# The inverse root of the LayerNorms on GpSimd beside VectorE's first product

## The chip, the cores and the metric

The kernel runs on one core of a Trainium2 chip. A core has a matmul engine (TensorE, PE in the profile), VectorE (DVE), ScalarE (ACT), GpSimd (POOL) and an engine that here only issues loads (SyncE, SP). Each engine takes its instructions in the order in which they stand in its own queue and waits on semaphores for the others. The metric is the time of one execution on the device, in microseconds (us); lower is better.

## The reference

Two transformer blocks of two layers each run one after the other on 256 tokens of width 1024, in float32. The first block normalises with RMS norms. The change concerns the second block only, whose residual stream passes four LayerNorms in each layer:

```python
def _layer_norm(x, g, b):
    xf = x.astype(jnp.float32)
    mu = jnp.mean(xf, -1, keepdims=True)
    var = jnp.mean(jnp.square(xf - mu), -1, keepdims=True)
    return ((xf - mu) * lax.rsqrt(var + LN_EPS) * g + b).astype(x.dtype)
...
    for l in range(DEPTH):          # DEPTH = 2
        x = _layer_norm(a * x + 0.5 * _swiglu(x, ffn1_w1[l], ...), ln1_g[l], ln1_b[l])
        mix = _token_mixing(x, w_in[l], ...)
        x = _layer_norm(a * x + mix, ln2_g[l], ln2_b[l])
        x = _layer_norm(a * x + _cross_attention(x, mem, ...), ln3_g[l], ln3_b[l])
        x = _layer_norm(a * x + 0.5 * _swiglu(x, ffn2_w1[l], ...), ln4_g[l], ln4_b[l])
```

Every product with a weight is a 128x512 matmul chain; to reach float32 accuracy each operand is split into a rounded part (hi) and a rest (lo), and three products are added.

## The kernel before

The tokens are two halves of 128 rows, `x0` (m = 0) and `x1` (m = 1), kept in SBUF. A weight tile is loaded by SP (tiles `raw`), cast to its hi part by ACT (line 329), and its lo part is made by DVE, raw minus hi (line 320, 1024 or 512 columns, both operands in SBUF).

A norm is made by `update` for one half. In order: the residual sum `x = a*x + acc` in two 512-column halves (line 657, `acc` in PSUM), the statistics of each half (line 661), their aggregate (line 666, giving mean and variance in `mv`), the inverse root `rsqrt` on a 128x1 column, and for each 512-column half the first product `(x - mean) * g` (line 679) and the second `x * r + b` (line 681). `rsqrt` has no table: it is an integer estimate and two polynomial steps, eight small VectorE instructions (lines 598, 599, 593, 601, 602, 593, 604, 605), each on the result of the one before.

The normed half is then turned by PE, in two groups of four 128x128 transposes (line 423), into PSUM; from there ACT copies the hi part (line 579) and DVE makes the lo part (line 580, one operand in PSUM). Those are the operands of the next matmuls (line 417).

How the halves are overlapped: `leave` runs the last products of a stage for m = 0 first, so that the norm of `x0` can run on DVE while PE does the products for m = 1; then it transposes `x0`. `gemm_first` begins the next stage with the first six weight tiles (`AHEAD`) for m = 0 while the norm of `x1` runs; then `arrive` ends that norm and transposes `x1`, and the m = 1 products follow. `hasten` gives the norm's instructions a high priority, and a list scheduler then fixes the order of each engine's queue; which other instructions stand between the steps of a norm is its result. The inverse roots of the RMS norms and of the small norms inside the token mixing use the same `rsqrt`.

Of the kernel before, what the change touches and what calls it, by code (L numbers as in the profile page):

```python
# [15 lines left out]
I32 = mybir.dt.int32  # L16
AF = mybir.ActivationFunctionType
ALU = mybir.AluOpType
AX = mybir.AxisListType

P = 128
# [8 lines left out]
LN_EPS = 1e-5  # L30
# [232 lines left out]
class Build:  # L263
# [321 lines left out]
    def rsqrt(self, var, n, eps):  # L585
# [19 lines left out]
        nc.vector.tensor_scalar(y, y, -0.5 * c2 ** 3, None, op0=ALU.mult)  # L605
        return y

    def fetch(self, dst, src):

        i = self.nc.gpsimd.dma_start(dst, src)  # L610
        if self.order is not None:
            self.after(i, self.recent[0])
# [34 lines left out]
    def update(self, m, acc, a, kind):  # L647

        nc, x = self.nc, self.x[m]
        st, mv = self.t("sm", [P, 32]), self.t("sm", [P, 32])  # L650
        halves = [slice(0, 512), slice(512, 1024)]
        for i, c in enumerate(halves):
            if acc is not None:
                if a is None:
                    ins = nc.vector.tensor_add(x[:, c], x[:, c], acc[i])  # L655
                else:
                    ins = nc.vector.scalar_tensor_tensor(x[:, c], x[:, c], a, acc[i], op0=ALU.mult, op1=ALU.add)  # L657
                if m == 1 and i == ORDER:
                    self.after(ins, self.done)
            if kind is not None:  # L660
                nc.vector.bn_stats(st[:, 6 * i:6 * i + 6], x[:, c])  # L661
            yield
        self.h[m] = x
        if kind is None:
            return
        nc.vector.bn_aggr(mv[:, :2], st[:, :12].rearrange("p (a b) -> p a b", b=6))
        if kind[0] == "rms":
            nc.vector.scalar_tensor_tensor(mv[:, 2:3], mv[:, 0:1], mv[:, 0:1], mv[:, 1:2], op0=ALU.mult, op1=ALU.add)
            r = self.rsqrt(mv[:, 2:3], 1, RMS_EPS)
            self.h[m] = self.t("b4", [P, 1024])  # L670
        else:
            r = self.rsqrt(mv[:, 1:2], 1, LN_EPS)
        yield
        for i, c in enumerate(halves):
            if kind[0] == "rms":
                self.done = nc.vector.scalar_tensor_tensor(self.h[m][:, c], x[:, c], r, kind[1][:, c],  # L676
                                                           op0=ALU.mult, op1=ALU.mult)
            else:
                nc.vector.scalar_tensor_tensor(x[:, c], x[:, c], mv[:, 0:1], kind[1][:, c],  # L679
                                               op0=ALU.subtract, op1=ALU.mult)  # L680
                self.done = nc.vector.scalar_tensor_tensor(x[:, c], x[:, c], r, kind[2][:, c],  # L681
                                                           op0=ALU.mult, op1=ALU.add)
            if kind[0] == "last":
                nc.sync.dma_start(self.a["out"][m * P:m * P + P, c], x[:, c])
            yield
# [1208 lines left out]
```

## Time and profile before

| | us |
|---|---|
| median of 3 runs | 2223.34 (2222.77 to 2224.21) |
| the profiled execution | 2224.18 |
| its span | 2222.4 |
| PE busy | 2186.5 |
| DVE busy | 1521.3 |
| ACT busy | 1078.4 |
| POOL busy | 113.7 |

The granted clock of PE is 0.999 over the span. The span is the time from the first to the last instruction of the profiled execution; the rest of its time lies around it. Busy shares tell how loaded an engine is, not what the end waits for; for that the chain and the waits are read, and then the timeline of the stretch in question. In a timeline a row with a count (x2, x8) stands for several instructions in a row, with the time from the first one's start to the last one's end, and consecutive instructions overlap a little.

### The profile page before, as it was taken

To read this page: it belongs to the slowest core of one execution; us is meant where nothing else is said; L and a number is where in the kernel's file an instruction comes from. 1 tells how busy PE (TensorE), PEld (TensorE's weight loads), DVE (VectorE), ACT (ScalarE), POOL (GpSimd) and SP (SyncE) were. 2 spreads that over 40 slices of the span, in tenths; PEclk is the share of its full clock that TensorE was granted. 3 is DMA by queue.
4 is the path that set the end of the run, shared out by engine and by line. 5 is a ranking of instruction groups with operands and counts; after the bars stand their busy time and mean duration, and the time that the engine had idled before them with its cause. 6 is when DMAs were issued, how large, how long until landed. Compare 5 with 4: busy or idle time off the path is not lost.

```text
span 2222.4 us, 30617 instructions
## 1 busy us (share of the span) xinstructions
PE 2186.5 (98%) x11454; PEld 1849.9 (83%) x11454; DVE 1521.3 (68%) x2456; ACT 1078.4 (49%) x1681; POOL 113.7 (5%) x191
## 2 busy tenths in 40 slices
PE   7999999999999999999999999999999999999998
PEld 6878888978888888889888888888888988897886
DVE  7677457778555555888877765575568887778555
ACT  5664344584444444456653444444435665444442
POOL 1000001000000000023000000000000310000000
PEclk9999999999999999999999999999999999999999
DMA  7355455445565555454556455555645444754561
GB/s 263 122 171 182 179 206 171 166 134 170 181 214 188 185 208 202 158 185 152 162 180 217 157 185 208 199 172 184 243 142 197 169 152 152 235 182 152 183 243 48
DMA packets 114709, 399.91 MB, mean 180 GB/s; under 512 B 13056, under 2 KB 13728, under 8 KB 114560
## 3 DMA queue, kind: packets, MB, share of 16 engines
q1 hardware_dynamic: 107712, 374.30, 48.7%
q0 software_dynamic: 6848, 23.66, 3.2%
q8 instruction: 90, 1.47, 0.3%
q14 instruction: 59, 0.48, 0.1%
HBM read 396.85 MB, written 1.05 MB: 179 GB/s over the span
## 4 chain that ended last, share of the span: by engine, by line
PE 86%; DVE 9%; ACT 3%; issue 2%; DMA 1%; SPq 0%; POOL 0%; DVEq 0%; ACTq 0%
PE ps L417 82%; PE ps L423 4%; DVE b L320 2%; DVE b L580 1%; DVE sm L661 1%; DVE x L679 1%; ACT b L329 0%; DVE x L657 0%; DVE x L681 0%; ACT b L579 0%; DVE sm L593 0%; DMA raw<-in_w_in_dram 0%; ACT b L1501 0%; DVE x L655 0%; ACT b L1553 0%
## 5 line engine op out<-in xcount | busy, mean ns | idle before, releaser
L417 PE MATMUL ps<-b,b 128*128 128x512 f32 (+7 forms) x10412 | 2088.6, 362 | 6.0 <-DVE b L320 2.4
L417 PEld LDWEIGHTS ps<-b,b 128*128 128x128 f32 (+2 forms) x10412 | 1734.3, 187 | 317.5 <-issue 10.9
L320 DVE TENSOR_TENSOR b<-raw,b 128x1024 fp32r<-128x1024 f32 (+3 forms) x738 | 843.4, 1179 | 47.8 <-PE ps L417 27.8
L329 ACT CAST b<-raw 128x1024 fp32r<-128x1024 f32 (+3 forms) x738 | 718.2, 1020 | 209.2 <-PE ps L417 135.8
L579 ACT CAST b<-ps 128x512 fp32r<-128x512 f32 (+2 forms) x188 | 101.1, 571 | 396.3 <-PE ps L423 310.7
L580 DVE TENSOR_TENSOR b<-ps,b 128x512 fp32r<-128x512 f32 (+2 forms) x188 | 118.8, 662 | 194.0 <-ACT b L579 193.3
L583 DVE SCALAR_TENSOR_TENSOR b<-ps,b 128x512 fp32r<-128x512 f32 (+1 forms) x64 | 39.1, 652 | 257.4 <-ACT b L582 257.4
L582 ACT ACTIVATE b<-ps 128x512 fp32r<-128x512 f32 (+1 forms) x64 | 33.1, 569 | 338.7 <-PE ps L423 338.7
L423 PE MATMUL ps<-cst,b 128*128 128x128 f32 (+1 forms) x810 | 106.9, 274 | 13.2 <-DVE b L676 11.5
L423 PEld LDWEIGHTS ps<-cst,b 128*128 128x128 f32 (+1 forms) x810 | 93.9, 140 | 25.4 <-DVE b L676 11.7
L610 POOL DMA_DIRECT2D b<-in_rows_dram x55 | 29.7, 543 | 1362.2 <-PE ps L417 899.3
L1553 ACT ACTIVATE b<-b,sm 128x128 f32<-128x128 f32 (+1 forms) x128 | 56.6, 446 | 8.0 <-DVE sm L828 7.8
L795 DVE TENSOR_TENSOR b<-b,ps 128x512 f32<-128x512 f32 (+1 forms) x48 | 30.8, 641 | 38.0 <-PE ps L417 36.7
L888 DVE TENSOR_TENSOR b<-ps,b 128x512 f32<-128x512 f32 x32 | 22.1, 689 | 27.1 <-PE ps L417 27.0
L890 ACT ACTIVATE b<-b 128x512 f32<-128x512 f32 x32 | 20.0, 629 | 41.8 <-DVE b L888 41.8
L661 DVE BATCH_NORM_STATS2 sm<-x 128x6 f32<-128x512 f32 x48 | 32.7, 688 | 4.1 <-DMA x<-in_x_dram 3.7
L1573 DVE TENSOR_TENSOR b<-b,sm 128x512 f32<-128x512 f32 x48 | 34.2, 740 | 0.3
L784 ACT ACTIVATE b<-ps 128x512 f32<-128x512 f32 x32 | 19.3, 604 | 27.4 <-PE ps L417 27.4
L793 ACT ACTIVATE b<-ps 128x512 f32<-128x512 f32 (+1 forms) x48 | 26.9, 561 | 10.4 <-PE ps L417 5.2
L794 DVE SCALAR_TENSOR_TENSOR b<-b,ps 128x512 f32<-128x512 f32 (+1 forms) x48 | 30.5, 636 | 0.0
L785 DVE SCALAR_TENSOR_TENSOR b<-ps,b 128x512 f32<-128x512 f32 x32 | 21.8, 685 | 12.5 <-ACT b L784 12.5
L871 DVE SCALAR_TENSOR_TENSOR b<-b,ps 128x512 f32<-128x512 f32 x32 | 21.7, 684 | 11.3 <-PE ps L417 11.3
(170 smaller groups left out, 744.6 us busy)
## 6 DMA issues: line engine op xcount, KB each, us to landing
raw<-in_ffn_w_dram SPq DMA_DIRECT2D x248, 512.0 KB, 5.6
raw<-in_w_in_dram SPq DMA_DIRECT2D x184, 512.0 KB, 4.7
raw<-in_w_up_dram SPq DMA_DIRECT2D x64, 512.0 KB, 5.2
raw<-in_w_down_dram SPq DMA_DIRECT2D x64, 512.0 KB, 5.0
b<-in_rows_dram POOLq DMA_DIRECT2D x19, 512.0 KB, 7.3
raw<-in_w_out_dram SPq DMA_DIRECT2D x16, 512.0 KB, 4.2
raw<-in_ffn_w_dram SPq DMA_DIRECT2D x32, 256.0 KB, 2.9
raw<-in_w_o_dram SPq DMA_DIRECT2D x16, 512.0 KB, 5.4
```

Source lines behind the costliest of these rows:

```text
L320: i = self.nc.vector.tensor_sub(lo[:, :n], r[:, :n], hi[:, :n].bitcast(F32))
L329: self.nc.scalar.copy(hi[:, :n], r[:, :n])
L417: i = self.nc.tensor.matmul(out, lhsT, rhs, start=start, stop=stop, skip_group_check=True)
L423: i = self.nc.tensor.transpose(out, in_, self.ident[:k, :k])
L579: nc.scalar.copy(hi, src)
L580: nc.vector.tensor_sub(lo, src, hi.bitcast(F32))
L582: nc.scalar.activation(hi, src, AF.Copy, scale=scale)
L583: nc.vector.scalar_tensor_tensor(lo, src, scale, hi.bitcast(F32), op0=ALU.mult, op1=ALU.subtract)
L661: nc.vector.bn_stats(st[:, 6 * i:6 * i + 6], x[:, c])
L795: nc.vector.tensor_mul(h[:, :w], r[:, :w], pss[1])
L1553: nc.scalar.activation(p[:, i], p[:, i], AF.Exp, scale=-1.0, bias=nm[:, at + i:at + i + 1], accum_out=den[:, at + i:at + i + 1])
L1573: e.tensor_mul(p, p, rinv[:, at:at + n].unsqueeze(2).broadcast_to((P, n, w)))
```

## The change

A second function makes the inverse root with the same eight steps on GpSimd, all as `tensor_scalar` on a 128x1 column; five of them take one or both scalars from a column in SBUF. `update` calls it for LayerNorms; the RMS norms keep the VectorE version. What follows it in the file moves down by 15 lines, so line 666 becomes 681, line 679 becomes 694 and line 681 becomes 696.

```diff
+    def rsqrt1(self, var, eps):
+
+        e = self.nc.gpsimd
+        c0, c1, c2 = 1.94246764, -1.3888181, 0.44639636
+        v, y, t = (self.t("sm", [P, 32])[:, :1] for _ in range(3))
+        e.tensor_scalar(v, var, eps, None, op0=ALU.add)
+        e.tensor_scalar(y.bitcast(I32), v.bitcast(I32), -0.5, 1596981248.0, op0=ALU.mult, op1=ALU.add)
+        e.tensor_scalar(t, y, y, v, op0=ALU.mult, op1=ALU.mult)
+        e.tensor_scalar(t, t, c1 / c2, t, op0=ALU.add, op1=ALU.mult)
+        e.tensor_scalar(y, t, c0 / c2, y, op0=ALU.add, op1=ALU.mult)
+        e.tensor_scalar(t, y, y, v, op0=ALU.mult, op1=ALU.mult)
+        e.tensor_scalar(y, t, -3 / c2 ** 2, y, op0=ALU.add, op1=ALU.mult)
+        e.tensor_scalar(y, y, -0.5 * c2 ** 3, None, op0=ALU.mult)
+        return y
...
         else:
-            r = self.rsqrt(mv[:, 1:2], 1, LN_EPS)
+            r = self.rsqrt1(mv[:, 1:2], LN_EPS)
```

In the order of the instructions 128 rows (16 norms of 8) leave DVE and 128 come to POOL. In the rows below a name is a tile with a running number (`sm` a small column, `b4` and `b2` SBUF tiles, `ps` a PSUM tile, `raw` a weight as loaded).

On POOL, the eight steps for `x1` of the first LN1, which stand right behind the eight for `x0`:

```order
L613 TENSOR_SCALAR sm_1678_8000<-sm_1670_7957 128x1
L614 TENSOR_SCALAR sm_1679_8001<-sm_1678_8000 128x1
L615 TENSOR_SCALAR sm_1680_8002<-sm_1679_8001,sm_1678_8000 128x1
L616 TENSOR_SCALAR sm_1680_8002<-sm_1680_8002 128x1
L617 TENSOR_SCALAR sm_1679_8001<-sm_1680_8002,sm_1679_8001 128x1
L618 TENSOR_SCALAR sm_1680_8002<-sm_1679_8001,sm_1678_8000 128x1
L619 TENSOR_SCALAR sm_1679_8001<-sm_1680_8002,sm_1679_8001 128x1
L620 TENSOR_SCALAR sm_1679_8001<-sm_1679_8001 128x1
```

Each step reads what the one before wrote; the first waits for the aggregate on DVE, and line 696 on DVE waits for the last.

On DVE, the same norm (`x1`, first LN1), before:

```order
L666 BN_AGGR sm_1670_7957<-sm_1669_7956 128x2
L679 SCALAR_TENSOR_TENSOR x1_83<-x1_83,sm_1670_7957,b4_1591_7604 128x512 x2
L598 TENSOR_SCALAR sm_1678_8000<-sm_1670_7957 128x1
L1071 TENSOR_TENSOR b2_1691_8058<-ps_1684_8021,b2_1362_6473 128x440
L599 TENSOR_SCALAR sm_1679_8001<-sm_1678_8000 128x1
L593 SCALAR_TENSOR_TENSOR sm_1680_8002<-sm_1679_8001,sm_1678_8000 128x1
L633 TENSOR_TENSOR b2_1698_8082<-b2_1691_8058,cst_81 128x32
L634 TENSOR_TENSOR b2_1699_8083<-b2_1691_8058,cst_81 128x16
L601 SCALAR_TENSOR_TENSOR sm_1680_8002<-sm_1680_8002 128x1
L635 TENSOR_TENSOR b2_1699_8083<-b2_1691_8058,cst_81 128x16
```

and after:

```order
L681 BN_AGGR sm_1670_7957<-sm_1669_7956 128x2
L694 SCALAR_TENSOR_TENSOR x1_83<-x1_83,sm_1670_7957,b4_1591_7604 128x512 x2
L696 SCALAR_TENSOR_TENSOR x1_83<-x1_83,sm_1679_8001,b4_1592_7606 128x512 x2
L320 TENSOR_TENSOR b4_1682_8016<-raw_1650_7858,b4_1681_8015 128x1024
L320 TENSOR_TENSOR b4_1686_8029<-raw_1651_7860,b4_1685_8028 128x1024
L1086 TENSOR_TENSOR b2_1691_8058<-ps_1684_8021,b2_1362_6473 128x440
L320 TENSOR_TENSOR b4_1689_8041<-raw_1654_7872,b4_1688_8040 128x1024
L598 TENSOR_SCALAR sm_1694_8065<-sm_1693_8062 128x2
L648 TENSOR_TENSOR b2_1698_8082<-b2_1691_8058,cst_81 128x32
```

The bias sum of the next stage (line 1071, 1086 after) and the rotary operations, which stood between the steps, now stand behind both products and the first conversions; nothing stands between line 694 and line 696.

On DVE at the first LN3, around the norm of `x1`, before:

```order
L681 SCALAR_TENSOR_TENSOR x0_82<-x0_82,sm_2468_11773,b4_2448_11711 128x512 x2
L657 SCALAR_TENSOR_TENSOR x1_83<-x1_83,ps_2445_11707 128x512
L580 TENSOR_TENSOR b4_2450_11714<-ps_2472_11809,b4_2449_11713 128x4x128
L661 BN_STATS sm_2470_11799<-x1_83 128x6
L580 TENSOR_TENSOR b4_2452_11716<-ps_2473_11816,b4_2451_11715 128x4x128
L666 BN_AGGR sm_2471_11800<-sm_2470_11799 128x2
L320 TENSOR_TENSOR b4_2465_11758<-raw_2406_11523,b4_2464_11757 128x1024
L679 SCALAR_TENSOR_TENSOR x1_83<-x1_83,sm_2471_11800,b4_2447_11709 128x512 x2
L598 TENSOR_SCALAR sm_2478_11845<-sm_2471_11800 128x1
L320 TENSOR_TENSOR b4_2475_11832<-raw_2425_11603,b4_2474_11831 128x1024
L599 TENSOR_SCALAR sm_2479_11846<-sm_2478_11845 128x1
L320 TENSOR_TENSOR b4_2482_11857<-raw_2428_11621,b4_2481_11856 128x1024
```

and after:

```order
L696 SCALAR_TENSOR_TENSOR x0_82<-x0_82,sm_2468_11773,b4_2448_11711 128x512 x2
L672 SCALAR_TENSOR_TENSOR x1_83<-x1_83,ps_2446_11708 128x512
L672 SCALAR_TENSOR_TENSOR x1_83<-x1_83,ps_2445_11707 128x512
L676 BN_STATS sm_2470_11799<-x1_83 128x6 x2
L580 TENSOR_TENSOR b4_2450_11714<-ps_2472_11809,b4_2449_11713 128x4x128
L681 BN_AGGR sm_2471_11800<-sm_2470_11799 128x2
L580 TENSOR_TENSOR b4_2452_11716<-ps_2473_11816,b4_2451_11715 128x4x128
L694 SCALAR_TENSOR_TENSOR x1_83<-x1_83,sm_2471_11800,b4_2447_11709 128x512 x2
L696 SCALAR_TENSOR_TENSOR x1_83<-x1_83,sm_2479_11846,b4_2448_11711 128x512 x2
L320 TENSOR_TENSOR b4_2465_11758<-raw_2406_11523,b4_2464_11757 128x1024
```

The conversions stood before and between the steps of the norm; now all of them stand behind its second products.

On PE at the first LN4, from the second group of `x1`'s transposes (`ps_2810`) on, before:

```order
L423 MATMUL ps_2810_13460<-cst_81,x1_83 128x128 x4
L417 MATMUL ps_2811_13467<-b4_2756_13213,b4_2749_13197 128x512
L417 MATMUL ps_2811_13467<-b4_2757_13214,b4_2749_13197 128x512
L417 MATMUL ps_2811_13467<-b4_2756_13213,b4_2749_13197 128x512
L417 MATMUL ps_2811_13467<-b4_2757_13214,b4_2749_13197 128x512
L417 MATMUL ps_2821_13510<-b4_2770_13265,b4_2749_13197 128x512
L417 MATMUL ps_2821_13510<-b4_2771_13266,b4_2749_13197 128x512
L417 MATMUL ps_2821_13510<-b4_2770_13265,b4_2749_13197 128x512
L417 MATMUL ps_2821_13510<-b4_2771_13266,b4_2749_13197 128x512
L417 MATMUL ps_2808_13440<-b4_2794_13393,b4_2751_13199 128x512
L417 MATMUL ps_2808_13440<-b4_2793_13392,b4_2751_13199 128x512
L417 MATMUL ps_2808_13440<-b4_2794_13393,b4_2751_13199 128x512
```

and after:

```order
L423 MATMUL ps_2810_13460<-cst_81,x1_83 128x128 x4
L417 MATMUL ps_2808_13440<-b4_2793_13392,b4_2751_13199 128x512
L417 MATMUL ps_2811_13467<-b4_2756_13213,b4_2749_13197 128x512
L417 MATMUL ps_2811_13467<-b4_2757_13214,b4_2749_13197 128x512
L417 MATMUL ps_2811_13467<-b4_2756_13213,b4_2749_13197 128x512
L417 MATMUL ps_2811_13467<-b4_2757_13214,b4_2749_13197 128x512
L417 MATMUL ps_2821_13510<-b4_2770_13265,b4_2749_13197 128x512
L417 MATMUL ps_2821_13510<-b4_2771_13266,b4_2749_13197 128x512
L417 MATMUL ps_2821_13510<-b4_2770_13265,b4_2749_13197 128x512
L417 MATMUL ps_2811_13467<-b4_2756_13213,b4_2750_13198 128x512 x2
L417 MATMUL ps_2811_13467<-b4_2759_13225,b4_2749_13197 128x512
L417 MATMUL ps_2811_13467<-b4_2760_13226,b4_2749_13197 128x512
```

The first matmul on `b4_2750`, the lo part that line 580 makes from the transposed `x1`, stands behind 14 matmuls before and behind 8 after (`b4_2749` is the hi part); six on `ps_2808` moved behind it.

## Rows read from the trace of the kernel before

**Rows 1.** The page: busy shares of the engines, and the chain by engine.

```profile
PE 2186.5 (98%) x11454; PEld 1849.9 (83%) x11454; DVE 1521.3 (68%) x2456; ACT 1078.4 (49%) x1681; POOL 113.7 (5%) x191
...
PE 86%; DVE 9%; ACT 3%; issue 2%; DMA 1%; SPq 0%; POOL 0%; DVEq 0%; ACTq 0%
```

**Rows 2.** Waits of PE: line <- releaser: total us, times, longest us.

```profile
PE ps L423 <- DVE x L681: 6.3, 7, 2.5
```

**Rows 3.** Timeline, DVE, first LN1: start, us, engine, line, operation, count, [idle <-releaser].

```profile
908.40 1.41 DVE L679 SCALAR_TENSOR_TENSOR x<-x,sm,b 128x512 f32<-128x512 f32 x2
909.73 0.15 DVE L598 TENSOR_SCALAR sm<-sm 128x1 f32<-128x1 f32 x1
...
911.38 0.75 DVE L681 SCALAR_TENSOR_TENSOR x<-x,sm,b 128x512 f32<-128x512 f32 x1
```

**Rows 4.** Timeline, POOL beside DVE, around 356 and 362 us.

```profile
355.82 1.29 DVE L580 TENSOR_TENSOR b<-ps,b 128x512 fp32r<-128x512 f32 x2 [4.75 <-ACT b L579]
...
356.05 0.24 POOL L909 TENSOR_TENSOR b<-cst,b 128x32 f32<-128x32 f32 x1
...
357.02 1.28 DVE L320 TENSOR_TENSOR b<-raw,b 128x1024 fp32r<-128x1024 f32 x1
...
357.18 1.30 POOL L908 TENSOR_TENSOR b<-cst,b 128x64 f32<-128x64 f32 x1
...
362.58 0.23 POOL L904 TENSOR_SCALAR sm<-b 128x8 f32<-128x8 f32 x1
```

**Rows 5.** Timeline, POOL, three dependent instructions one after the other.

```profile
1046.73 0.31 POOL L635 TENSOR_TENSOR b<-b,cst 128x64 f32<-128x64 f32 x1
1047.12 0.46 POOL L638 TENSOR_TENSOR h<-b,b 128x128 f32<-128x128 f32 x1
1047.64 0.29 POOL L1195 COPY b<-h 128x128 f32<-128x128 f32 x1
```

**Rows 6.** Groups by line on POOL: line, shapes, count, busy us, mean ns, idle before.

```profile
L1883 POOL MEMSET const-float32-1.0<- 128x1 f32 x1 | 0.1, 98 | 0.0
```

**Rows 7.** Timeline, DVE and PE, second half of the first LN1.

```profile
917.87 1.42 DVE L679 SCALAR_TENSOR_TENSOR x<-x,sm,b 128x512 f32<-128x512 f32 x2
...
921.32 1.42 DVE L681 SCALAR_TENSOR_TENSOR x<-x,sm,b 128x512 f32<-128x512 f32 x2
...
927.40 0.68 DVE L580 TENSOR_TENSOR b<-ps,b 128x512 fp32r<-128x512 f32 x1
...
923.93 13.31 PE L417 MATMUL ps<-b,b 128*128 128x512 f32 x60 [0.48 <-DVE b L320]
```

**Rows 8.** Timeline, PE, first half of the first LN2.

```profile
1220.92 0.63 PE L423 MATMUL ps<-cst,x 128*128 128x128 f32 x4 [0.24 <-DVE x L681]
```

**Rows 9.** Timeline, DVE and PE, first LN3.

```profile
1275.48 1.42 DVE L679 SCALAR_TENSOR_TENSOR x<-x,sm,b 128x512 f32<-128x512 f32 x2
...
1279.46 1.42 DVE L681 SCALAR_TENSOR_TENSOR x<-x,sm,b 128x512 f32<-128x512 f32 x2
...
1280.36 1.29 PE L423 MATMUL ps<-cst,x 128*128 128x128 f32 x8 [2.53 <-DVE x L681]
1281.66 11.18 PE L417 MATMUL ps<-b,b 128*128 128x512 f32 x48
```

**Rows 10.** Timeline, DVE and PE, second half of the first LN4.

```profile
1474.19 1.41 DVE L679 SCALAR_TENSOR_TENSOR x<-x,sm,b 128x512 f32<-128x512 f32 x2
...
1477.69 1.42 DVE L681 SCALAR_TENSOR_TENSOR x<-x,sm,b 128x512 f32<-128x512 f32 x2
...
1482.50 1.28 DVE L580 TENSOR_TENSOR b<-ps,b 128x512 fp32r<-128x512 f32 x2
...
1479.83 12.55 PE L417 MATMUL ps<-b,b 128*128 128x512 f32 x53
```

**Rows 11.** Timeline, DVE, the last norm of the program.

```profile
2214.72 1.42 DVE L679 SCALAR_TENSOR_TENSOR x<-x,sm,b 128x512 f32<-128x512 f32 x2
...
2217.70 1.42 DVE L681 SCALAR_TENSOR_TENSOR x<-x,sm,b 128x512 f32<-128x512 f32 x2
```

## The prediction

> **What bounds the kernel now.** I read the shares of busy time first, then the chain that ended last, then the waits of the matmul engine, then the stretches around the LayerNorms. The matmul engine PE is busy 98% of the span and holds 86% of the chain; VectorE (DVE) holds 9% of it and GpSimd (POOL) is busy 5% [rows 1]. So a microsecond taken from VectorE is worth nothing as such. It counts only where PE stands idle until a norm's result arrives. Of such waits for the norm's last product (line 681) there are seven, 6.3 us together, 2.5 the longest [rows 2]. They are the whole prize that a shorter norm can win inside the span, with one more norm at the very end. A norm that gets longer has no such limit: behind each there is a PE that has only a few matmuls left to do.
>
> Of the sixteen LayerNorms (4 in each of 2 layers, for 2 halves of 128 tokens) the first one shows the shape. The two first products (line 679) start at 908.40, the first of the eight small steps at 909.73, the second products (line 681) at 911.38 [rows 3]. From start to start that is 2.98: 1.33 for the products and 1.65 for eight steps, 0.206 each. What the change is worth is decided by what this 2.98 becomes; I call it the gap.
>
> **What the steps cost on GpSimd.** The sixteen chains of eight move as they are; the order shows 128 more rows on POOL and 128 fewer on DVE. The queue of POOL is empty of other work at every chain, so nothing is queued behind them. The trace of before has no 128x1 arithmetic on POOL. The nearest row is a TENSOR_SCALAR on 128x8, 0.23 [rows 4]. Between dependent POOL instructions lie 0.08 (1046.73 + 0.31 to 1047.12) and 0.06 (1047.12 + 0.46 to 1047.64) [rows 5]. That makes 0.23 + 0.07 = 0.30 a step. From below the nearest is a MEMSET of one column, 0.10 [rows 6], so 0.17; from above the 128x128 product of 0.46 [rows 5], so 0.53, should the five steps that take a scalar from memory be dear. I take 0.30, the row of the same kind and nearly the same size.
>
> The Trainium skill (GPSIMD Engine Reference, section 3.1) has an elementwise operation 1.96 times slower on GpSimd than on VectorE and names two software dispatches for each instruction. No run here shows this for one column; an estimate from it is 1.96 x 0.206 = 0.40 a step, and the sum below would be 7 us higher.
>
> **Can they run beside the first products?** Here the trace speaks against the change. A POOL product on 32 columns takes 0.24 at 356.05, while DVE runs line 580, which has one operand in PSUM [rows 4]. At 357.18 the same kind of work on 64 columns takes 1.30: DVE is in line 320 from 357.02 to 358.30, with both operands in SBUF, and POOL ends 0.18 after it [rows 4]. POOL is held until the DVE instruction is done. Line 679 also has two tensors in SBUF (x and the gain row g), so it belongs to the second kind.
>
> The Trainium skill (SBUF — State Buffer, section "Who interferes with whom") states this as a rule: a VectorE instruction with two SBUF inputs locks out, for its whole length, a GpSimd instruction that reads SBUF. By that rule the trace agrees (1.30 against 0.24), and the overlap that the change wants is mostly lost.
>
> So of the eight steps one gets through between the two products and one as the second ends, about 0.11 late (the small step needs less than the 64 columns that came 0.18 late). Six remain behind: new gap = 1.41 + 0.11 + 6 x 0.30 = 3.32. Against 2.98 this is +0.34 for a norm on whose path nothing else lies. And DVE, in order, stands idle meanwhile.
>
> **What the changed order does.** In before, other DVE work was placed between the small steps and filled the time; in after nothing stands between the products, and that work comes behind. So the price has to be taken place by place.
>
> *LN1, twice (two layers), +1.5 each.* First half: DVE is 0.34 later. Second half: the gap was 3.45 (917.87 to 921.32) [rows 7] and becomes 3.32, -0.13. But line 1071 (0.53 by start to start) and four small operations of the rotary step (some 0.1 each), which stood inside it, now stand between the norm and line 580, +0.9. Line 580 ended at 927.40 + 0.68 = 928.08 [rows 7] and will end near 929.2. PE needs its result after 20 matmuls in before: 923.93 + 20 x 0.222 (13.31 / 60 [rows 7]) = 928.36, just in time. In after only 17 stand ahead of it, so PE waits until 929.2 and still owes three (0.66): 929.2 - 928.36 + 0.66 = 1.5. Together 3.0.
>
> *LN2, twice, +0.1 each.* PE waits 0.24 for the first half at 1220.92 [rows 8]. The gap shrinks there too, since a weight conversion leaves it, but the transposes stand 3 to 4 matmuls earlier; a tenth is left by my count. Together 0.2.
>
> *LN3, twice, +2.4 each.* First half: the gap was 1279.46 - 1275.48 = 3.98, with a residual sum and a statistic of the other half inside; it becomes 3.32, and PE's wait of 2.53 shrinks by 0.66 [rows 9]. The second half takes that back and more. In before a conversion (line 320) stood ahead of the second norm's first products; in after it stands behind that whole norm. From 1275.48 it now comes after: gap 3.32, products 1.33, four sums and statistics of 0.6 each, two of line 580 at 0.6, the aggregate 0.12, which gives 1283.85 for the second norm; then its gap 3.32 and products 1.33, so the conversion starts at 1288.5 and, at the 1.17 to 1.2 that line 320 takes on average, ends near 1289.7. (I take 0.6, a little under the half of 1.33, for an operation on one half of a row, from start to start.) PE wanted that operand 24 matmuls of 0.233 (11.18 / 48) after 1281.66, at 1287.25 [rows 9]: +2.4. Together 4.8.
>
> *LN4 of the first layer, +1.7.* DVE comes 0.34 later by the first half and 0.18 earlier by the second (1477.69 - 1474.19 = 3.50 to 3.32). The first line 580 ended near 1483.2 (1482.50, two in 1.28, the first 0.68), and will near 1483.4 [rows 10]. PE needed it after 14 matmuls of 0.237 (12.55 / 53): 1479.83 + 3.32 = 1483.15. In after it stands behind 8, so six are owed once it comes: 1483.4 + 1.42 = 1484.8.
>
> *The last norm, +0.3.* From 2214.72 to 2217.70 is 2.98 again, with no work of PE behind it [rows 11].
>
> Sum: 3.0 + 0.2 + 4.8 + 1.7 + 0.3 = +10.0. The profiled execution took 2224.18, so it would take 2234.2; it lies 0.84 above the median of 2223.34, so against the median: **2233.3**.
>
> At some twelve of the norms the end moves with the gap (LN1 and LN3 both halves and both layers, eight; LN2 first half, two; LN4; the last). So 0.1 us of gap is worth 1.2 us, and the cost of a step counts 6 x 12 = 72 times: 0.01 more for each is 0.7 us.
>
> **Rivals.**
>
> *POOL is not held (not slower).* Line 679 has a scalar pointer as its third operand, and its form is none of those beside which a hold was seen; if POOL's first step got in ahead of each product, or this form left POOL its port, the eight steps would run from the start: gap 0.12 + 8 x 0.30 = 2.52, 0.80 less than forecast. 10.0 - 12 x 0.80 = +0.4, so 2223.7: the moved order eats the gain. It decides from a gap under about 2.9. For it: 0.24 beside line 580. Against: 1.30 beside line 320.
>
> *Held, but short steps.* At 0.17 a step the gap is 1.52 + 6 x 0.17 = 2.54, again 10.0 - 9.4 = +0.6, 2223.9. From 0.22 a step up it is beyond 2227.8.
>
> *Both.* The gap is then 0.12 + 8 x 0.17 = 1.48, all waits of [rows 2] shrink by up to 1.5, and the tail too; bounded by those waits the time would be about 2218.
>
> *Dear steps.* At 0.53 a step: +6 x 0.23 x 12 = 16.6 more, 2250; at 0.40, 2240.5. For it: five of eight steps read their scalars from memory, and the row of 0.23 may not. This is more of the same sign.
>
> *The change does not do what it says* is excluded by the order: all 128 rows stand on POOL.
>
> **How the numbers follow.** About 0.2% (4.45 us) is what a measurement of this kernel can tell from no change: faster means below 2218.9, slower above 2227.8. Chances: forecast with 0.22 to 0.37 a step 0.55, dear steps 0.15, not held 0.13, short steps 0.12, both 0.05. Slower: 0.55 + 0.15 = 0.70; same: 0.13 + 0.12 less 0.01 for a better case = 0.24; faster 0.06. The range leaves out the case of both and the dearest steps (above 0.43, some 0.1): 2222 to 2243.
>
> **What would show it.** In the profile of the changed kernel, line 694 to line 696 should be near 3.3 from start to start, with DVE idle and put down to POOL; of POOL's eight rows the first should be stretched to about 0.7 beside line 694 and the last six stand behind it, about 0.30 apart. PE's waits should grow for lines 580 and 320 rather than for line 696, at LN1 and LN3. A gap near 2.5 with unstretched POOL rows would prove the first rival; rows further apart than 0.4 the dear steps. I would be wrong in another way if the gap is 3.3 and the time unchanged: then PE had more cover behind the norms than I counted.

## The result and the profile after

The changed kernel takes 2240.65 us (median of 6 runs, 2240.18 to 2241.12) against 2223.78 for the kernel before beside it: a ratio of 1.0074, 95% interval 1.0064 to 1.0084. That is 16.9 us slower. Forecast were +10, 2233.3 with a range up to 2243. The profiled span is 2238.5.

Busy times and instructions of the engines, from the page of the changed kernel:

```profile
PE 2188.3 (98%) x11454; PEld 1851.0 (83%) x11454; DVE 1503.6 (67%) x2328; ACT 1077.9 (48%) x1681; POOL 168.7 (8%) x319
```

VectorE is 17.7 us less busy than in [rows 1], which is what was taken from it; nothing of that comes back. Where the time went is seen in the waits of PE (line, what it waited for: total us, times, longest):

```profile
PE ps L423 <- DVE x L696: 10.8, 10, 2.3
PE ps L417 <- DVE b L580: 7.3, 7, 1.8
PE ps L417 <- DVE b L320: 4.6, 5, 1.7
```

The waits for the norm's second product (line 681, now 696) were 6.3 in seven [rows 2] and are 10.8 in ten. The waits for line 580, the lo part of the transposed norm, were 2.0 us and are 7.3; those for the conversions (line 320) were 2.4 and are 4.6.

The first norm, as in [rows 3]: VectorE's two products of the changed kernel,

```profile
906.69 1.42 DVE L694 SCALAR_TENSOR_TENSOR x<-x,sm,b 128x512 f32<-128x512 f32 x2
910.49 0.75 DVE L696 SCALAR_TENSOR_TENSOR x<-x,sm,b 128x512 f32<-128x512 f32 x1 [2.38 <-POOL sm L620]
```

and between them the eight steps on GpSimd:

```profile
906.75 0.78 POOL L613 TENSOR_SCALAR sm<-sm 128x1 f32<-128x1 f32 x1 [53.22 <-DVE sm L681]
907.61 0.55 POOL L614 TENSOR_SCALAR sm<-sm 128x1 int32<-128x1 int32 x1
908.27 0.34 POOL L615 TENSOR_SCALAR sm<-sm,sm 128x1 f32<-128x1 f32 x1
908.71 0.27 POOL L616 TENSOR_SCALAR sm<-sm 128x1 f32<-128x1 f32 x1
909.08 0.26 POOL L617 TENSOR_SCALAR sm<-sm,sm 128x1 f32<-128x1 f32 x1
909.45 0.34 POOL L618 TENSOR_SCALAR sm<-sm,sm 128x1 f32<-128x1 f32 x1
909.88 0.26 POOL L619 TENSOR_SCALAR sm<-sm,sm 128x1 f32<-128x1 f32 x1
910.23 0.22 POOL L620 TENSOR_SCALAR sm<-sm 128x1 f32<-128x1 f32 x1
```

From the first product to the second it is 3.80, forecast was 3.32, before 2.98. VectorE waits 2.38 for GpSimd's last step. The first two steps are held: 0.78 and 0.55 instead of about 0.2, and the second is over at 908.16, 1.47 after the products began (forecast 1.52). Behind them stand the six others, as expected, but at 0.37 from start to start (908.27 to 910.49 in six), not 0.30: they last 0.22 to 0.34 and lie about 0.10 apart. Over all 16 norms the gap is 3.78 to 3.80, but for the second halves at LN2 and LN3 (3.49 and 3.41). There another VectorE instruction stands between the aggregate and the products, so GpSimd's first steps begin ahead of the products and other steps are held by them.

The second half of the first LN1 on PE (in [rows 7] there was no wait for line 580):

```profile
921.83 1.32 PE L423 MATMUL ps<-cst,x 128*128 128x128 f32 x8 [0.34 <-DVE x L696]
922.90 4.07 PE L417 MATMUL ps<-b,b 128*128 128x512 f32 x17
928.74 11.55 PE L417 MATMUL ps<-b,b 128*128 128x440 f32 x52 [1.76 <-DVE b L580]
```

After the transposes PE has 17 matmuls and then waits 1.76 for line 580. At the first LN3 (compare [rows 9]),

```profile
1282.23 1.94 PE L423 MATMUL ps<-cst,x 128*128 128x128 f32 x8 [2.33 <-DVE x L696]
1283.99 6.62 PE L417 MATMUL ps<-b,b 128*128 128x512 f32 x25
1292.33 2.79 PE L417 MATMUL ps<-b,b 128*128 128x512 f32 x11 [1.72 <-DVE b L320]
```

the wait for the product is 2.33 (2.53 before) and a new one of 1.72 stands behind it, for the conversion that now comes after the second norm. PE's clock falls here too: from the end of the first wait on its granted clock is 0.5 (1.2 GHz) for 3.4 us, and the eight transposes take 1.94, against 1.29 in [rows 9]. That is not what makes the stage longer: behind it PE waits 1.72 for VectorE, whose work between the two norms runs without a pause. At LN4 (compare [rows 10]),

```profile
1485.21 2.14 PE L417 MATMUL ps<-b,b 128*128 128x512 f32 x8
1488.87 3.47 PE L417 MATMUL ps<-b,b 128*128 128x512 f32 x14 [1.52 <-DVE b L580]
```

eight matmuls follow the transposes and then a wait of 1.52. And the last norm, compare [rows 11]:

```profile
2228.30 1.41 DVE L694 SCALAR_TENSOR_TENSOR x<-x,sm,b 128x512 f32<-128x512 f32 x2
2232.08 1.42 DVE L696 SCALAR_TENSOR_TENSOR x<-x,sm,b 128x512 f32<-128x512 f32 x2 [2.37 <-POOL sm L620]
```

Laid along the program, the offset between the two profiles at the first product of `x0` tells each stage's price:

| stage | forecast, both layers | measured, layer 1 and 2 | sum |
|---|---|---|---|
| LN1 | 3.0 | 2.9 + 2.9 | 5.8 |
| LN2 | 0.2 | 0.9 + 0.9 | 1.7 |
| LN3 | 4.8 | 2.5 + 2.4 | 4.9 |
| LN4 (first layer) | 1.7 | 2.7 | 2.7 |
| last norm, both halves | 0.3 | 1.0 | 1.0 |
| sum | 10.0 | | 16.1 |

The two spans differ by 16.1 as well. (The offset is -1.7 before the first LayerNorm and 1.7 more again behind the last; these cancel. I take them as belonging to the single executions, which no run tests.)

### The profile page after: what moved, and what is told of

It reads as the page before. It is cut to its first block, busy times and chain, and to the rows that moved or that the text cites. A ratio compares the mean times of both kernels' runs of the same rounds, so it can differ in the third digit from the quotient of the medians.

```text
span 2238.5 us, 30655 instructions
## 1 busy us (share of the span) xinstructions
PE 2188.3 (98%) x11454; PEld 1851.0 (83%) x11454; DVE 1503.6 (67%) x2328; ACT 1077.9 (48%) x1681; POOL 168.7 (8%) x319
## 3 DMA queue, kind: packets, MB, share of 16 engines
q8 instruction: 90, 1.47, 0.3%
## 5 line engine op out<-in xcount | busy, mean ns | idle before, releaser
L696 DVE SCALAR_TENSOR_TENSOR x<-x,sm,b 128x512 f32<-128x512 f32 x32 | 22.6, 749 | 36.6 <-POOL sm L620 36.6
L613 POOL TENSOR_SCALAR sm<-sm 128x1 f32<-128x1 f32 x16 | 11.8, 738 | 312.7 <-DVE sm L681 312.7
L423 PE MATMUL ps<-cst,x 128*128 128x128 f32 x128 | 20.0, 290 | 10.9 <-DVE x L696 10.8
```

The lines of the kernel that those rows point to most:

```text
L423: i = self.nc.tensor.transpose(out, in_, self.ident[:k, :k])
```

## Experiments

All times are medians beside runs of the kernel before on the same chip; the difference to that is what is compared. The kernel before took 2223.8 beside the one-input, the six-step, the two-step and the first interleaved run, 2224.4 beside the runs of one half of the tokens and of one half of the interleaving, and 2224.5 beside the last three (the filled LN3, the second interleaved run, all norms).

### Is GpSimd held by VectorE's two-input products?

The changed kernel with the first product replaced by a statistics instruction, which stands behind the aggregate by an order-only dependency:

```diff
-        nc.vector.bn_aggr(mv[:, :2], st[:, :12].rearrange("p (a b) -> p a b", b=6))
+        aggr = nc.vector.bn_aggr(mv[:, :2], st[:, :12].rearrange("p (a b) -> p a b", b=6))
...
-                nc.vector.scalar_tensor_tensor(x[:, c], x[:, c], mv[:, 0:1], kind[1][:, c],
-                                               op0=ALU.subtract, op1=ALU.mult)
+                self.after(nc.vector.bn_stats(st[:, 16 + 6 * i:22 + 6 * i], x[:, c]), aggr, "NoSync")
```

> The changed kernel with line 694, the first product with two tensors from SBUF, replaced by a statistics instruction on the same 512 columns (one tensor from SBUF, 0.69 us each as against 0.7): (x - mean) * g is left out. Theory 'held': GpSimd's steps wait for each of VectorE's two-input instructions, and the six steps behind them are what the gap consists of. Without the hold all eight run at 0.36 to 0.37 from the start: gap near 3.0 instead of 3.80, the first GpSimd row near 0.25 instead of 0.77, and with 12 norms on the path 12 x 0.8 = 9.6 us less than the changed kernel, near 2231. Rival 'slow steps alone': the first rows are long because the start from VectorE's semaphore is slow; gap stays 3.8, time near 2240.

2230.07, 6.3 over before (ratio 1.0029, 1.0018 to 1.0040) and 10.6 below the changed kernel. VectorE (lines 694 and 695) and the first two steps on GpSimd, at the first norm:

```profile
906.84 1.23 DVE L694 BATCH_NORM_STATS2 sm<-x 128x6 f32<-128x512 f32 x2
909.85 1.42 DVE L695 SCALAR_TENSOR_TENSOR x<-x,sm,b 128x512 f32<-128x512 f32 x2 [1.78 <-POOL sm L620]
...
907.02 0.22 POOL L613 TENSOR_SCALAR sm<-sm 128x1 f32<-128x1 f32 x1 [53.07 <-DVE sm L681]
907.33 0.19 POOL L614 TENSOR_SCALAR sm<-sm 128x1 int32<-128x1 int32 x1
```

The steps that took 0.78 and 0.55 take 0.22 and 0.19 beside an instruction with one input from SBUF, and the gap is 3.01. Over the 16 norms it is 2.98 to 3.02. So the hold is real, and it costs 0.8 us for each norm. The Trainium skill (SBUF — State Buffer, "Who interferes with whom") says that a VectorE instruction with at most one SBUF input does not contend with GpSimd, and that one with two contends with a GpSimd instruction that reads SBUF; 0.22 against 0.78 agrees.

What decides more is the other half of the result. The gap is here what it was in before where nothing lay in it, and the time is still 6.3 us longer. PE's waits in this run:

```profile
PE ps L417 <- DVE b L580: 9.4, 10, 1.8
PE ps L423 <- DVE x L695: 5.4, 6, 1.6
```

The product is waited for 5.4 us (6.3 before [rows 2]); line 580 for 9.4 us, against 2.0. The same LN1 place as above reads

```profile
921.50 3.82 PE L417 MATMUL ps<-b,b 128*128 128x512 f32 x15
927.10 13.15 PE L417 MATMUL ps<-b,b 128*128 128x440 f32 x59 [1.78 <-DVE b L580]
```

with a wait of 1.78, as in the changed kernel (1.76). That points to the moved order, with the gap at its old length: work that stood between VectorE's steps, where it cost next to nothing, now stands between the norm and line 580, and PE has fewer matmuls placed in front of its result. This kernel has nearly the order of the changed one, but not wholly: its scheduler moved some operations around the norms and behind LN1. The next two kernels have exactly that order on VectorE and on PE.

### How much time is a microsecond of gap worth?

Two kernels with the changed kernel's order on VectorE and fewer steps on GpSimd.

```diff
-        e.tensor_scalar(y, t, -3 / c2 ** 2, y, op0=ALU.add, op1=ALU.mult)
-        e.tensor_scalar(y, y, -0.5 * c2 ** 3, None, op0=ALU.mult)
```

> The changed kernel with six GpSimd steps for each norm: the last correction and the final factor are left out, so r is not the inverse root. The order on VectorE is that of the changed kernel. Gap 3.80 - 2 x 0.37 = 3.06, that is nearly the 2.98 of before. Theory 'gap and moved order both cost': 2240.6 - 12 x 0.74 = 2231.8, so about 8 us over before are the price of work that stood inside the gap and now stands behind it. Rival 'the gap alone': time back near 2224.5 to 2226.

2227.95, 4.1 over before (ratio 1.0016, 1.0007 to 1.0025). It was neither of the two numbers, because the gap was not the expected one: the sixth instruction's result is read by nobody, so five are on the path, and VectorE's two products stand

```profile
907.90 1.41 DVE L692 SCALAR_TENSOR_TENSOR x<-x,sm,b 128x512 f32<-128x512 f32 x2
910.58 1.42 DVE L694 SCALAR_TENSOR_TENSOR x<-x,sm,b 128x512 f32<-128x512 f32 x2 [1.27 <-POOL sm L617]
```

2.68 apart, not 3.06. This gap is shorter than any of before (2.98 at the least), and the kernel is still 4.1 us slower than before; what is left as the cause is the moved order, which is exactly that of the changed kernel. From 3.80 to 2.68 the time falls by 12.7: 11.3 us for each us of gap.

The second kernel stops after the first two steps:

> The changed kernel with the first two GpSimd steps only (the estimate by bits; polynomial and correction left out). Gap about 1.6: both steps are let through beside the products. Theory 'gap and moved order both cost': 2240.6 - 12 x 2.2 = 2214 if the slope held, but no wait falls below nothing, so 2216 to 2222. Rival 'moved order alone': the gap doesn't matter, time above 2230. Rival 'the gap alone': 2224 less the waits of before on the norm's products (6.3 us and the tail's 1.4), 2216.

2214.26, 9.6 below before (ratio 0.9958, 0.9945 to 0.9970).

```profile
908.48 1.41 DVE L688 SCALAR_TENSOR_TENSOR x<-x,sm,b 128x512 f32<-128x512 f32 x2
909.98 1.41 DVE L690 SCALAR_TENSOR_TENSOR x<-x,sm,b 128x512 f32<-128x512 f32 x2
```

The gap is 1.50 here and 1.32 to 1.50 over the norms. The time lies below the 2216 to 2222 that were expected: PE's waits for the product are gone (6.3 us), and its waits for the conversions fell by 0.9 us and its own busy time by 2.3 as well, which I had not counted; those for line 580 rose by 1.6. All differences to before by gap:

| gap, us | 3.80 | 3.0 (other product) | 2.68 | about 1.4 |
|---|---|---|---|---|
| over before, us | +16.9 | +6.3 | +4.1 | -9.6 |

They lie near one line of 11 us for each us. At a gap of 2.98, that of before, the line stands some 7 us above before, which again is put down to the moved order. With its order the change would have had to bring the gap under about 2.3 to gain anything, and eight steps of 0.37 cannot, held or not.

### Which half of the tokens?

The same call for one half only, `if m == 0` or `if m == 1`.

```diff
-            r = self.rsqrt1(mv[:, 1:2], LN_EPS)
+            r = self.rsqrt1(mv[:, 1:2], LN_EPS) if m == 0 else self.rsqrt(mv[:, 1:2], 1, LN_EPS)
```

> GpSimd takes the inverse root for the first half of the tokens only (x0, eight norms); x1 keeps VectorE's eight steps. Theory 'gap and moved order, place by place': the gap of x0 is 3.8, and what is moved there is a residual sum and a statistic at LN3; the conversions and the bias sum stay inside the gap of x1. Four PE waits of about 0.5 to 1.4 (LN1, LN2, LN3, LN4) in each layer: 5 to 8 us over before, 2229 to 2232. Rival 'only the second half matters, the m = 0 half has cover': within 2 us of before.

2230.24, 5.8 over before (ratio 1.0029, 1.0018 to 1.0041). Waits of PE for the product and for line 580:

```profile
PE ps L423 <- DVE x L696: 9.9, 8, 2.4
PE ps L417 <- DVE b L580: 2.0, 3, 0.7
```

> GpSimd takes the inverse root for the second half only (x1); x0 keeps VectorE's steps. Here the moved work is largest (line 1071, the conversions at LN2 and LN3), so the larger part of 16.9: 8 to 12 us, 2232 to 2236. If both halves add, this run and the one for x0 together give 16.9; if the two norms of one stage stand in one queue and share a wait, less than that.

2232.69, 8.3 over before (ratio 1.0042, 1.0029 to 1.0055):

```profile
PE ps L423 <- DVE x L696: 8.0, 9, 2.5
PE ps L417 <- DVE b L580: 4.3, 6, 1.1
```

With the first half alone the waits that grow are those for the product, 9.9 us instead of 6.3; line 580 is waited for 2.0 as in before. That is 3.6 us. About as much again in this profile is PE's clock: behind the wait of 2.35 for the norm at LN3 the granted clock is 0.5 (1.2 GHz) for 3.4 us in each layer, and the transposes and the 48 matmuls behind that wait take 1.6 to 1.8 us longer than in [rows 9]. The profile of before waits 2.53 at that place and shows no such stretch, so the wait alone does not decide it. With the second half alone waits for line 580 come in (4.3), and the clock falls at LN3 in both layers too. Together they make 14.1, a little under 16.9; the intervals of the two (about 2.5 us each) don't tell that from a sum.

### Can the idle time be filled again?

The changed kernel idles 2.4 us in each norm. At LN3 one conversion is brought back into that time for `x1`.

```diff
+                if m == 1 and i == 0 and kind[3] == 3:
+                    self.after(self.done, getattr(self, "last_lo", None), "NoSync")
```

`kind[3]` is the number of the norm here, `last_lo` the conversion that was issued last, and `after` an order-only dependency.

> The changed kernel with one order-only dependency: at LN3, for x1 alone, the second products stand behind the next conversion (line 320), which comes back into the gap, and the one after it between the two second products. All else is as in the changed kernel. Theory 'moved order': PE's waits of 1.72 and 1.34 us for that conversion at the two LN3 go, and x1's transposes, which did not wait there, have cover: about 3 us less than the changed kernel's 2240.65, 2237.7, although the gap of that norm grows by a microsecond or more (the conversion has two SBUF inputs and holds GpSimd again). Rival 'the gap alone': two longer gaps, 2240 to 2243.

2240.33, 15.8 over before (ratio 1.0073, 1.0060 to 1.0087): no gain that can be told from the changed kernel's 16.9, and within the 2240 to 2243 of the rival. GpSimd's third step and PE behind it at the first LN3:

```profile
1287.58 2.38 POOL L615 TENSOR_SCALAR sm<-sm,sm 128x1 f32<-128x1 f32 x1
...
1293.76 1.43 PE L417 MATMUL ps<-b,b 128*128 128x512 f32 x5 [0.66 <-DVE b L320]
...
1298.50 4.83 PE L417 MATMUL ps<-b,b 128*128 128x512 f32 x20 [0.33 <-DVE b L580]
```

The wait for the conversion falls from 1.72 to 0.66, as it should if the moved order is the cause there. But a wait of 0.33 for line 580 appears, and on GpSimd the third step is held for 2.38, through both products and the conversion, so that the gap of this norm is 4.46 instead of 3.41 and the norm ends later. From the transposes of `x0` at LN3 to those at LN4 the profile is 0.4 us shorter (189.98 against 190.38). My 3 us were wrong: I had not counted that the next conversion becomes the late one. So the run shows what the wait of 1.72 was for, but not that the time comes back with it. What the profile adds is that this idle time can't be filled with work of two SBUF inputs, since that work stops the very steps that VectorE is waiting for.

### A version that is faster than both

If eight dependent steps leave VectorE idle between one and the next, the two first products can stand there, with all steps on VectorE:

```diff
+    def rsqrt2(self, var, eps, cover):
...
+        e.tensor_scalar(y.bitcast(I32), var.bitcast(I32), -0.5, 1596981248.0, op0=ALU.mult, op1=ALU.add)
+        i = e.tensor_scalar(v, var, eps, k, op0=ALU.add, op1=ALU.mult)
+        i = self.then(cover(0), i)
+        i = self.then(e.scalar_tensor_tensor(t, y, v, y, op0=ALU.mult, op1=ALU.mult), i)
+        i = self.then(cover(1), i)
+        self.then(e.scalar_tensor_tensor(t, t, c1 / c2 * k, t, op0=ALU.add, op1=ALU.mult), i)
+        e.scalar_tensor_tensor(y, t, c0 / c2 * k ** 2, y, op0=ALU.add, op1=ALU.mult)
+        e.scalar_tensor_tensor(t, y, v, y, op0=ALU.mult, op1=ALU.mult)
+        e.scalar_tensor_tensor(y, t, 1.5 * c2 / k ** 2, y, op0=ALU.add, op1=ALU.mult)
...
```

`cover(i)` is the first product of half i, `then` an order-only dependency, and k = -(0.5 c2^3)^(1/7) scales v so that the final factor of -0.5 c2^3 is 1. The first estimate is taken from the variance itself, not from v, so the first two steps don't depend on each other.

> The kernel before with the inverse root kept on VectorE, but in seven steps instead of eight (the final factor is folded into v), the first two independent of one another, and the two first products placed by order-only dependencies between the steps, so that they fill the time in which a step waits for the one before. Gap of an undisturbed norm 0.07 + 0.07 + 0.66 + 0.1 + 0.66 + four steps of 0.2 = 2.35 instead of 2.98. PE's waits on the norm's second product (6.3 us, seven) shrink by up to 0.63 each where they are that long: 2 x 0.63 + 5 x 0.25 and the tail 0.63, 3 us in all: 2220.5. Rival 'moved order': if VectorE's other work is again pushed behind the norm, as in the changed kernel, the time stays at 2224 or rises by a few us.

2217.54, 6.3 below before (ratio 0.9971, 0.9960 to 0.9982); a second time:

> The interleaved kernel once more, beside the two others on the same chip: 2217.5 if its 6.3 us hold.

2217.31, 7.2 below (0.9970, 0.9958 to 0.9982). VectorE at the first LN3, first half (line 693 is the first product, 702 the second):

```profile
1274.33 0.15 DVE L614 TENSOR_SCALAR sm<-sm 128x1 int32<-128x1 int32 x1
1274.40 0.14 DVE L615 TENSOR_SCALAR sm<-sm 128x1 f32<-128x1 f32 x1
1274.46 0.74 DVE L693 SCALAR_TENSOR_TENSOR x<-x,sm,b 128x512 f32<-128x512 f32 x1
1275.12 0.21 DVE L617 SCALAR_TENSOR_TENSOR sm<-sm,sm 128x1 f32<-128x1 f32 x1
1275.25 0.75 DVE L693 SCALAR_TENSOR_TENSOR x<-x,sm,b 128x512 f32<-128x512 f32 x1
1275.91 0.15 DVE L619 SCALAR_TENSOR_TENSOR sm<-sm 128x1 f32<-128x1 f32 x1
1276.10 0.16 DVE L620 SCALAR_TENSOR_TENSOR sm<-sm,sm 128x1 f32<-128x1 f32 x1
1276.29 0.22 DVE L621 SCALAR_TENSOR_TENSOR sm<-sm,sm 128x1 f32<-128x1 f32 x1
1276.55 0.16 DVE L622 SCALAR_TENSOR_TENSOR sm<-sm,sm 128x1 f32<-128x1 f32 x1
1276.74 1.41 DVE L702 SCALAR_TENSOR_TENSOR x<-x,sm,b 128x512 f32<-128x512 f32 x2
```

The gap is 1276.74 - 1274.33 = 2.41 from the first step, and 2.28 from the first product; before it was 3.98 with 1.2 us of other work inside [rows 9]. Two independent steps cost 0.07 each, and the step between the products 0.13; the dependent ones still cost 0.19 to 0.26. PE waits

```profile
PE ps L417 <- DVE b L580: 3.6, 5, 0.8
PE ps L423 <- DVE x L702: 2.2, 3, 1.0
```

2.2 us for the product instead of 6.3, and 3.6 for line 580 instead of 2.0. The gain was twice the 3 us that were expected. The waits on the product fell by 4.1 us and those on the conversions by 0.9, those on line 580 rose by 1.6, and the tail is 0.7 shorter; PE's own busy time is 1.8 less.

Each half of that change alone:

> Half of the interleaved kernel: VectorE's eight steps as before, but the two first products are placed behind the first and the second step. Gap of an undisturbed norm 0.07 + 0.65 + 0.13 + 0.65 + six steps of 0.206 = 2.74 against 2.98: by 11 us of time for each us of gap, 2.6 us less, 2221.2. Rival: the gain of 6.3 us came from placement alone, by way of what the scheduler put elsewhere; then 2218.

2222.54, 1.9 below before (ratio 0.9993, 0.9984 to 1.0002).

> The other half: seven steps, the first two independent, and the products ahead of them as before. Gap 1.33 + 0.07 + six steps of 0.206 = 2.64: 3.7 us less by the same slope, 2220.1. Together the two halves should give about the 6.3 us of the interleaved kernel. Rival: the placement alone carries it, and this is within 1 us of before.

2222.71, 1.7 below (ratio 0.9993, 0.9984 to 1.0003). Neither can be told from no change by itself, and 2222.71 is a miss: 2220.1 was expected. Gaps of an undisturbed norm are 2.65 and 2.66 in them, as expected (2.74, counted from the first step, and 2.64). Their gains add up to 3.6, against 6.3 to 7.2 for both together. A part of that lies in PE's clock. The seven-step kernel at the first LN3:

```profile
1278.39 1.29 PE L423 MATMUL ps<-cst,x 128*128 128x128 f32 x8 [2.25 <-DVE x L696]
1279.69 12.79 PE L417 MATMUL ps<-b,b 128*128 128x512 f32 x48
```

The same 48 matmuls took 11.18 in before [rows 9]. From 1279.99 on the granted clock is 0.5 (1.2 GHz) for 3.4 us, behind a wait of 2.25 for the norm; at the second layer's LN3 it is the same, and in the kernel with the placement alone as well (12.51 and 12.56 for the 48). That is some 3 us in each of the two profiles. In the interleaved kernel the wait there is 0.96, and the granted clock stays at 1.0 (2.4 GHz). All the runs fit: the mean granted clock is 0.997 or 0.998 in all 22 runs of the two halves, and 0.999 in 10 of the 13 interleaved ones. The kernel before has both: 2222.98 is the median of its runs at 0.999, 2224.94 of those at 0.997. So the two halves gained on the gap and lost some of it to the clock. How much the scheduler, which lays out the rest anew in each kernel, adds to that, these runs don't say.

The same root in the first block's RMS norms:

> The interleaved kernel with its seven-step root in the RMS norms of the first block too (there without products between, since an RMS norm has none ahead of the root): eight norms, each about 0.2 to 0.3 us shorter. If PE waits for them as for the LayerNorms: 2217.5 - 8 x 0.25 = 2215.5. Rival: they have cover, 2217.5.

2216.91, 7.6 below before (ratio 0.9969, 0.9956 to 0.9981): not to be told from the interleaved kernel's 7.2 beside it. Those norms have cover, or the gain is too small for this measurement.

## Why the prediction was right, and where a size was off

*What bounds the kernel.* Right: VectorE lost 17.7 us of busy time and the kernel became slower; the waits of PE and the tail moved the end.

*Two of eight steps get through beside the products.* Right in the count and the size at 12 of the 16 norms: the second was over 1.47 after the start, forecast 1.52. The other four are the second halves of LN2 and LN3. That it is a hold, and not a slow start, the one-input run shows (0.22 instead of 0.78).

*The step at 0.30.* This is the term that was mis-sized. It measured 0.37: the row on 128x8 that I took [rows 4] has the kind and nearly the size, but the steps with a scalar read from memory last 0.27 and those with two 0.34, and the distance between dependent steps was 0.10, not the 0.07 of [rows 5]. I had named the scalars as the reason for dear steps and given that 0.15. The Trainium skill's ratio (GPSIMD Engine Reference, section 3.1) pointed to 0.40; measured it is 0.37 / 0.206 = 1.80. The page's 1.96 is for an addition of 2048 elements, so its nearness on one column may be chance. The forecast gap of 3.32 became 3.80. The 0.48 more at twelve norms is 5.8 us, of the 6.9 that were missing; the slope of 12 that I worked out was 11 when measured. That the total fits so well is in part luck, since the places don't fit alike: by this count LN1 and LN3, four norms each, should each have cost 1.9 us more than forecast, and cost 2.8 and 0.1 more (at the second halves of LN3 the gap was only 3.41).

*The moved order.* Right in kind and about in size. Forecast without the gap it was about 6 us (10.0 less 12 x 0.34); the one-input run, at the gap of before, measured 6.3, and the line through the runs 7. Of the places, LN3 came out near the forecast (4.9, forecast 4.8), though with a first gap 0.46 longer than I had it, so not by the sum that I gave. LN4 came out to the matmul (eight, then a wait), at 2.7 instead of 1.7 by the larger gap of its two halves. LN1 was dearer (5.8 for 3.0), of which the larger gap of both halves gives 1.9, and LN2, where I left a tenth, showed 0.9 in each layer: the transposes that had been moved forward met a gap of 3.79, not 3.32, which gives 0.5. The rest of both stays open.

*The rivals.* 'POOL is not held' is refuted by the held rows and by the one-input run. But its arithmetic is worth a look: without the hold the gap was 3.0, not the 2.52 that I gave it, again since the steps are dearer; and at that gap the one-input run is 6.3 us over before, where the rival had 2223.7. 'Dear steps' was half true, at 0.37 where I had set its limit.

## What to carry to other kernels

Before moving a chain of tiny dependent steps to an idle engine, compare the two engines step by step (0.37 against 0.206 here), and count as overlap only the steps that really run beside something (two of eight here). Look first at what stands between the steps now: a chain with holes is free room for other work, and taking the chain away throws that work out onto the path (6 to 7 us here). Filling those holes with the work that waits for the chain's end, on the same engine, made this kernel faster by 6 to 7 us. And where differences of a few us are compared, compare the granted clock of the stretches too: two halves of that change seemed to bring next to nothing, while the profile of each shows some 3 us lost at half the clock.

## What the runs showed of the hardware

A 128x1 instruction on GpSimd took 0.19 to 0.22 with constants, 0.26 to 0.27 with one scalar column and 0.34 with two, and dependent ones lay about 0.10 apart.

The hold is not always ended by the next boundary between two VectorE instructions. The first step, waiting beside the first product, was done before the second had run (0.78 in all). A step with two scalar columns that met the first of two products did not get in between: the third step took 1.32 at the second halves of LN3 in the changed kernel, over both products, and 2.38 in the filled one, over two products and a conversion that stood back to back; in the six-step kernel the last step met the second products and took 1.40 at all sixteen norms. Whether it is the two columns that make the difference no run tests.

On VectorE a 128x1 step that depends on nothing in flight cost 0.07 from start to start, a dependent one 0.19 to 0.26.

Behind a wait of PE of 2.3 us at LN3 the granted clock was 0.5 (1.2 GHz) for 3.4 us in several kernels, and 48 matmuls took 12.5 to 12.8 us instead of 11.18. Where PE next waited for VectorE, as in the changed kernel, that cost nothing more; where it did not, it cost some 1.6 us each time. In the profile of before a wait of 2.53 was followed by no such stretch; why, no run shows.
